# One buffer for the raw down weights of the first gated network, beside a ring of three for its up weights

## The chip, the cores and the metric

The kernel runs on one core of a Trainium2 chip. A core has a matrix engine (TensorE, "PE" in the profile; "PEld" is its weight load), a vector engine (VectorE, "DVE"), a scalar engine (ScalarE, "ACT"), a general engine (GpSimd, "POOL") and a queue processor (SyncE, "SP") that issues most of the transfers from main memory into the on-chip buffer. The engines run side by side, each works through its own instructions in order, and they wait for each other by semaphores. The metric is the device time of one execution in microseconds; lower is better.

## The reference

A decoder trunk of two layers on one sequence of 512 positions with 1024 channels, all in float32. The first layer mixes tokens with a state-space model, the second with attention. Behind each mixer stands a gated feed-forward network with 2816 hidden channels. Every sub-layer is preceded by a normalisation whose shift, scale and gate come from a conditioning vector `c` through a matrix `ada_w`. What matters here is the gated network:

```python
def conv_ffn(h, w_up, conv_w, conv_b, w_down):
    up = h @ w_up
    a, b = jnp.split(up, 2, axis=-1)
    S = a.shape[1]
    ap = jnp.pad(a, ((0, 0), (CONV_W - 1, 0), (0, 0)))
    a_conv = conv_b
    for i in range(CONV_W):
        a_conv = a_conv + ap[:, i:i + S] * conv_w[i]
    return (jax.nn.silu(a_conv) * b) @ w_down
```

With `h` 512 x 1024, `w_up` 1024 x 5632 and `w_down` 2816 x 1024. In `reference`, layer 0 calls `s5_mixer`, then `conv_ffn`; layer 1 calls `fox_mixer`, then `conv_ffn`; a last `rmsnorm` follows.

## The kernel before

Activations are kept transposed: channels on the 128 partitions, the 512 positions along the free axis. A float32 product is made from three products of halves: each operand is split into a high part and the remainder (`w_hi`, `w_lo` for weights), and TensorE computes hi·hi, hi·lo and lo·hi into the same accumulator (`mms`, L275). The split of a weight costs one ACT copy (`w_hi`, L258) and one DVE subtraction (`w_lo`, L259), both in `put_parts`.

A weight tile first lands in a buffer named `raw` (`raw()`, its transfer is issued on the SP queue at L167). These buffers are a ring of `RAW = 3`; a buffer is free again when ACT and DVE have read it. The `w_hi` and `w_lo` tiles are rings of `WB = 5`, free again when TensorE has used them.

The gated network (`ffn`) walks over 22 blocks `f` of 128 hidden channels. A block needs two up-weight tiles of 128 x 1024 (512 KB each). For most blocks of the first network `quarters` computes the up product with seven quarter products instead of eight (Strassen–Winograd): from the two raw tiles `a` and `b` it makes on DVE the sums `c` and `d` (L499), splits `a`, `c`, `d` (128 x 1024 each) and a quarter of `b`, called `a22` (128 x 512), and then runs 84 matmuls of 256 columns (`times`, L529), whose results ACT copies out (L536) and DVE combines (L499). A causal convolution (L578, L580), a SiLU (L583) and the gate product (L590) follow. Blocks 0, 1, 2, 3, 6, 11 and 17 (`plain`) take the ordinary product instead.

The blocks stand in five groups, (4, 4, 5, 4, 5). From the second group on, each block `f` is followed by one or two of the eight down products of the *previous* group (`down(q - 1, ...)`): each loads one raw tile of the down weights (128 x 512, 256 KB, for a group of four; 128 x 640, 320 KB, for a group of five), splits it, runs 12 or 15 matmuls of 512 columns, and adds the result into the residual `h` (L343). So a *step* of this loop loads `a` and `b`, then one or two down tiles, which the texts below call d1 and d2. There are 32 such down tiles, 14 pairs and 4 single ones. The eight down products of the last group follow behind the loop.

Beside that, the first gated network carries background work: the parameters of later sub-layers (`ada_units`), one transfer of 512 KB on the POOL queue and one DVE reduction (L228) for each unit, two units in most steps (`self.tick(ticks)`). The second gated network calls `ffn` with `ticks=0`: it has no such work.

The order of instructions on each engine, SP's transfers among them, is laid down when the program is built: a planner takes them in program order as operands and buffers come free in its own estimate of time, and the engines then keep to that order. Only the beginning of the state-space layer is ordered by hand (`manual_schedule`).

Pools of on-chip memory: `const` lives through the whole program; `s5p` lives through the state-space layer; `ffn0` and `ffn1` through the gated networks. `const` holds, among others, the pack `first` (the conditioning vector and small tables of the state-space layer, 176 floats to a partition) and `ones`, a 128 x 128 tile of ones. `ones` is the weight-side operand of the first normalisation (L1081), and one column of it is used in `rms_stats` (L361) throughout.

Of the kernel before, what the change touches and what calls it, by code (L numbers as in the profile page):

```python
# [8 lines left out]
F32 = mybir.dt.float32  # L9
F32R = mybir.dt.float32r  # L10
I32 = mybir.dt.int32
AF = mybir.ActivationFunctionType
# [5 lines left out]
P = 128  # L18
D = 1024
KT = D // P  # L20
# [22 lines left out]
FIRST = (("c", (KT,)), ("s5_prm", (3, G // 2)), ("s5_eye", (64,)), ("s5_causal", (L,)))  # L43
# [15 lines left out]
class Trunk:  # L59
# [6 lines left out]
    def __init__(self, tc, io, ctx):  # L66
        self.tc, self.nc, self.io, self.ctx = tc, tc.nc, io, ctx
        nc = self.nc
        pool = lambda name, bufs, **k: ctx.enter_context(tc.tile_pool(name=name, bufs=bufs, **k))
        self.const = pool("const", 1)  # L70
        self.act = pool("act", 1)
        self.wpool = pool("wpool", 3)
        self.tmp = pool("tmp", 2)
        self.small = pool("small", 2)
        self.dram = pool("dram", 1, space=DRAM)
        self.mm = pool("mm", 4, space=PSUM)
        self.aux = pool("aux", 4, space=PSUM)
        self.bg = []
        self.acc = None
        self.pending = None  # L80
        self.normed, self.evac, self.copied, self.squared = [], [], [], []
        self.sums = {}

        self.first = self.load_pack("first", FIRST)
        self.c = self.first["c"]
        self.ones = self.const.tile([P, P], F32, name="ones")
        nc.vector.memset(self.ones, 1.0)
        self.sc = self.const.tile([P, KT], F32, name="sc")
        nc.scalar.activation(self.sc, self.c, AF.Silu)
        self.scd = self.dram.tile([KT, P], F32, name="scd")  # L90

        self.sel = self.const.tile([P, 6], F32, name="sel")
        nc.gpsimd.memset(self.sel, 0.0)
        for q in range(4):
            for c in (q, 4 + q % 2):
                nc.gpsimd.memset(self.sel[32 * q:32 * q + 1, c:c + 1], 1.0)
        self.par = [self.const.tile([P, 24], F32, name=f"par{i}") for i in range(4)]
        self.ga = [self.const.tile([P, KT], F32, name=f"ga{i}") for i in range(4)]

    def load_pack(self, name, parts):  # L100

        t = self.const.tile([P, sum(math.prod(s) for _, s in parts)], F32, name=name)
        self.nc.sync.dma_start(t, self.io[name])
        out, a = {}, 0
        for n, s in parts:
            w = math.prod(s)
            v = t[:, a:a + w]
            out[n] = v.rearrange("p (a b) -> p a b", b=s[1]) if len(s) == 2 else v
            a += w
        return out  # L110

    def load_rest(self):
        for n, v in self.load_pack("rest", REST).items():
            setattr(self, n, v)

    def load_x(self, pool):
# [46 lines left out]
            yield  # L163

    def raw(self, shape, src, n=0):
        t = self.wpool.tile(shape, F32, name="raw", tag=("raw", "w_hi", "w_lo")[n], bufs=(RAW, WB, WB)[n])
        self.nc.sync.dma_start(t, src)  # L167
        return t
# [184 lines left out]
    def rms_stats(self, cols):  # L353

        nc = self.nc
        nb = (cols.stop - cols.start) // P
        parts = [t[:, cols] for t in (self.acc, self.acc_last)]
        ps = self.aux.tile([P, nb], F32, name="aux")
        for n, part in enumerate(parts):
            for b in range(nb):  # L360
                nc.tensor.matmul(  # L361
                    ps[:, b:b + 1], part[:, b * P:(b + 1) * P], self.ones[:, 0:1],
                    start=(n == 0 and b == 0), stop=(n == 1), skip_group_check=True,
                )
        return self.inv_root(ps, nb)
# [196 lines left out]
    def ffn(self, i, l, x, nxt, ticks=0, plain=None):  # L562

        nc, tc = self.nc, self.tc
        with tc.tile_pool(name=f"ffn{l}", bufs=1, reuse_waits="tile") as pool:
            self.bgpool = pool
            conv = pool.tile([P, 4, FT], F32, name="conv_wb")
            nc.sync.dma_start(conv, self.io["conv"][l])
            cw, cb = conv[:, :3], conv[:, 3]
            groups = QGROUPS[l] if plain else GROUPS  # L570
            first = [sum(groups[:q]) for q in range(len(groups) + 1)]
            keep, g = {}, {}

            def gated(m, ps, cols):
                f = m // 2
                if m % 2 == 0:
                    t = pool.tile([P, S], F32, name="conv", bufs=2 if plain else 3)
                    nc.scalar.activation(t, ps, AF.Identity, bias=cb[:, f:f + 1], scale=cw[:, 2, f:f + 1])  # L578
                    for d in (1, 2):
                        c = nc.vector.scalar_tensor_tensor(  # L580
                            t[:, d:], ps[:, :S - d], cw[:, 2 - d, f:f + 1], t[:, d:], op0=ALU.mult, op1=ALU.add
                        )
                    nc.scalar.activation(t, t, AF.Silu)  # L583
                    keep[f] = t
                    if plain and f >= groups[0]:
                        self.evac = [c.ins]
                        self.tick(ticks)
                    return
                t = keep.pop(f)
                nc.vector.tensor_tensor(t, t, ps, ALU.mult)  # L590
                q = sum(f >= n for n in first[1:])
                j = f - first[q]
                if not j:
                    tag = f"{q % 2}" if plain else ""
                    g[q] = [pool.tile([P, groups[q], S], F32R, name=n, tag=n + tag) for n in ("ghi", "glo")]
                hi, lo = g[q]
                self.put_parts(hi[:, j, :], lo[:, j, :], t)

            after, y = nxt
            up = lambda fs, **k: self.product(  # L600
                self.io["w_up"][l], range(2 * fs[0], 2 * fs[-1] + 2), KT, x, gated,
                ticks=0 if plain else ticks, **k
            )
            last = len(groups) - 1
            down = lambda q, ms, **k: self.product(
                self.io["w_down"][l][:, :, first[q]:first[q + 1], :], ms, groups[q], g[q],
                self.add_residual(i, q == last), after=after, ticks=0 if plain else ticks, **k
            )
            todo = []
            for q, n in enumerate(groups):  # L610
                fs = range(first[q], first[q + 1])
                if not plain:
                    up(fs, head=0 if q else 3)
                    if q < last:
                        down(q, range(KT))
                    continue
                for j, f in enumerate(fs):
                    if f == 0:
                        up([0, 1], head=3)
                        todo.append(self.forms_x(pool, x))  # L620
                    elif f in plain:
                        if f > 1:
                            up([f])
                        for _ in range(4):
                            if todo and next(todo[0], True):
                                todo.pop()
                    else:
                        while todo:
                            if next(todo[0], True):
                                todo.pop()  # L630
                        self.quarters(pool, l, f, x, gated)
                    if q:
                        down(q - 1, range(j * KT // n, (j + 1) * KT // n))
                        self.tick(ticks)
            down(last, range(KT), tail=TAIL if plain else 2, tail_pool=(pool, 4))
        return y
# [121 lines left out]
class S5(Trunk):  # L758
# [292 lines left out]
    def s5(self, i, nxt):  # L1051
        nc, tc = self.nc, self.tc
# [4 lines left out]
        with ExitStack() as stack:  # L1057
            spool = lambda name, st: st.enter_context(tc.tile_pool(name=name, bufs=1, reuse_waits="tile"))
            keep = spool("s5p", stack)
            self.s5q = spool("s5q", stack)  # L1060
            with ExitStack() as start:
                tp = spool("s5t", start)
# [10 lines left out]
                with tc.manual_schedule(engines={ENG.PE, ENG.Activation, ENG.DVE, ENG.SP}):  # L1073
# [4 lines left out]
                    for k in range(KT):  # L1078
                        sq = self.tmp.tile([P, S], F32, name="nm_t")
                        nc.scalar.activation(sq, self.h[:, k, :], AF.Square)  # L1080
                        nc.tensor.matmul(ps, self.ones, sq, start=(k == 0), stop=(k == KT - 1))  # L1081
                    rows = self.tmp.tile([P, S], F32, name="nm_t")
                    nc.scalar.activation(rows, ps, AF.Copy)
                    stats = self.aux.tile([P, NB, P], F32, name="aux")
# [527 lines left out]
```

## Time and profile before

| what | value |
|---|---|
| device time, median of 3 runs | 1247.41 us (1247.23 to 1250.16) |
| profiled execution: device time | 1250.96 us |
| profiled execution: span shown in the profile | 1249.2 us |
| TensorE busy, share of the span | 1217.2 us, 97% |
| VectorE busy | 1010.6 us, 81% |
| ScalarE busy | 609.2 us, 49% |
| bytes moved | 183.83 MB |

The span runs from the first to the last instruction of the profiled execution. "Busy" is the time in which an engine executes; a row of a view names the line of the code, the engine, the operation, the output and the inputs, and then durations. An arrow (`<-`) behind an idle time names what the engine was waiting for. The granted clock is the share of the full rate that TensorE was allowed in a stretch.

In the span the state-space layer takes about the first 260 us, the first gated network lies from about 265 to 635 us, attention to about 890 us and the second gated network behind it.

### The profile page before, as it was taken

What the parts mean: (1) busy time and instruction counts of PE and PEld (TensorE: products, weight loads), DVE (VectorE), ACT (ScalarE), POOL (GpSimd) and SP (SyncE); (2) the same over time, 40 slices, a digit from 0 to 9 for tenths busy, and PEclk for the clock granted to TensorE, in tenths of its full rate; (3) what the DMA queues carried; (4) which work ended last, traced back from release to release, by engine and by line L of the source; (5) the groups of instructions that cost most, each with busy time, mean ns of one, the idle gap of its engine ahead of it and who ended that gap; (6) DMA issues with size and microseconds to landing.
All of it is one profiled execution on the core that took longest, in us unless ns stands there. A gap on an engine that the chain in (4) does not pass through costs nothing.

```text
span 1249.2 us, 20558 instructions
## 1 busy us (share of the span) xinstructions
PE 1217.2 (97%) x7921; PEld 1039.6 (83%) x7921; DVE 1010.6 (81%) x1871; ACT 609.2 (49%) x1137; POOL 83.3 (7%) x143
## 2 busy tenths in 40 slices
PE   7999999999998999999999999999999999999997
PEld 2566678898988888889899877878989999999987
DVE  7888986779888888899788587885899887888855
ACT  3544465335444444444553565654366544555443
POOL 0000000100000000000000233431000000000000
PEclk9999989999998999999999999999999999999999
DMA  9677668521343544453525444432213332323331
GB/s 365 221 240 241 218 196 289 204 96 34 126 170 114 186 152 150 159 194 127 162 102 203 163 142 148 154 106 85 87 51 110 118 111 83 110 92 115 100 94 68
DMA packets 74385, 183.83 MB, mean 147 GB/s; under 512 B 23231, under 2 KB 25631, under 8 KB 73263
## 3 DMA queue, kind: packets, MB, share of 16 engines
q1 hardware_dynamic: 68239, 161.02, 38.1%
q0 software_dynamic: 5760, 20.97, 5.0%
q8 instruction: 62, 1.02, 0.3%
q10 hardware_dynamic: 288, 0.52, 0.1%
q14 instruction: 36, 0.29, 0.1%
HBM read 175.57 MB, written 6.92 MB: 146 GB/s over the span
## 4 chain that ended last, share of the span: by engine, by line
PE 70%; issue 14%; DVE 8%; DMA 5%; ACT 1%; POOL 1%; SPq 0%; DVEq 0%; POOLq 0%; ACTq 0%
PE mmp L275 29%; PE mmp L529 14%; PE aux L529 6%; PE mmp L1141 4%; PE mmp L1332 2%; DVE w_lo L259 2%; PE aux L947 2%; DMA raw<-in_w_up 2%; PE mmp L1170 2%; PE aux L1036 1%; PE aux L1471 1%; PE mmp L186 1%; PE aux L1028 1%; DVE ada_raw L228 1%; PE mmp L1081 1%
## 5 line engine op out<-in xcount | busy, mean ns | idle before, releaser
L258 ACT ACTIVATE w_hi<-raw 128x1024 fp32r<-128x1024 f32 (+5 forms) x205 | 175.9, 865 | 145.5 <-PE mmp L275 61.2
L259 DVE TENSOR_TENSOR w_lo<-raw,w_hi 128x1024 fp32r<-128x1024 f32 (+5 forms) x205 | 207.0, 1017 | 49.1 <-ACT w_hi L258 48.8
L275 PE MATMUL mmp<-ghi,w_hi 128*128 128x512 f32 (+1 forms) x392 | 146.4, 373 | 0.0
L275 PE MATMUL mmp<-glo,w_hi 128*128 128x512 f32 (+1 forms) x392 | 146.1, 373 | 0.0
L275 PE MATMUL mmp<-ghi,w_lo 128*128 128x512 f32 (+1 forms) x392 | 145.9, 372 | 0.0
L275 PE MATMUL mmp<-a_hi,w_hi 128*128 128x512 f32 (+1 forms) x376 | 139.0, 372 | 1.5 <-ACT a_hi L414 1.5
L275 PE MATMUL mmp<-a_hi,w_lo 128*128 128x512 f32 (+1 forms) x376 | 136.6, 364 | 0.0
L275 PE MATMUL mmp<-a_lo,w_hi 128*128 128x512 f32 (+1 forms) x376 | 136.4, 363 | 0.0
L529 PE MATMUL mmp<-w_hi,w_lo 128*128 128x256 f32 x396 | 111.9, 283 | 3.6 <-DVE w_lo L259 3.6
L529 PE MATMUL mmp<-w_hi 128*128 128x256 f32 x396 | 112.3, 284 | 2.8 <-ACT w_hi L258 2.1
L529 PE MATMUL mmp<-w_lo,w_hi 128*128 128x256 f32 x396 | 111.5, 282 | 0.0
L258 ACT ACTIVATE w_hi<-sums 128x1024 fp32r<-128x1024 f32 x74 | 77.5, 1057 | 32.9 <-DVE sums L499 31.4
L536 ACT ACTIVATE nm_h<-mmp 128x256 f32<-128x256 f32 x99 | 37.5, 381 | 111.3 <-PE mmp L529 111.0
L259 DVE TENSOR_TENSOR w_lo<-sums,w_hi 128x1024 fp32r<-128x1024 f32 x74 | 90.2, 1219 | 0.5 <-ACT w_hi L258 0.4
L275 PEld LDWEIGHTS mmp<-ghi,w_lo 128*128 128x128 f32 x392 | 73.9, 189 | 14.2
L343 DVE SCALAR_TENSOR_TENSOR h<-mmp,par,h 128x512 f32<-128x512 f32 (+1 forms) x100 | 68.2, 683 | 20.6 <-PE mmp L275 20.1
L275 PEld LDWEIGHTS mmp<-ghi,w_hi 128*128 128x128 f32 x392 | 74.0, 189 | 12.9
L275 PEld LDWEIGHTS mmp<-glo,w_hi 128*128 128x128 f32 x392 | 73.9, 189 | 12.8
L275 PEld LDWEIGHTS mmp<-a_hi,w_hi 128*128 128x128 f32 x376 | 70.5, 189 | 14.1 <-issue 2.6
L275 PEld LDWEIGHTS mmp<-a_hi,w_lo 128*128 128x128 f32 x376 | 70.9, 189 | 11.8 <-DVE w_lo L259 0.6
L529 PEld LDWEIGHTS mmp<-w_hi 128*128 128x128 f32 x396 | 76.4, 193 | 3.6 <-ACT w_hi L258 2.5
L275 PEld LDWEIGHTS mmp<-a_lo,w_hi 128*128 128x128 f32 x376 | 71.1, 189 | 9.9
(314 smaller groups left out, 3065.2 us busy)
## 6 DMA issues: line engine op xcount, KB each, us to landing
raw<-in_w_up SPq DMA_DIRECT2D x88, 512.0 KB, 3.5
raw<-in_ada_w SPq DMA_DIRECT2D x40, 512.0 KB, 6.1
ada_raw<-in_ada_t POOLq DMA_DIRECT2D x40, 512.0 KB, 4.0
raw<-in_w_down SPq DMA_DIRECT2D x32, 320.0 KB, 3.2
nf<-nfd SPq DMA_DIRECT2D x8, 1152.0 KB, 6.5
raw<-in_fox_qk SPq DMA_DIRECT2D x16, 512.0 KB, 3.8
raw<-in_w_down SPq DMA_DIRECT2D x24, 256.0 KB, 3.0
raw<-in_w_down SPq DMA_DIRECT2D x16, 384.0 KB, 3.3
```

The costliest lines, as they stand in the source:

```text
L186: self.last_mm = nc.tensor.matmul(ps[32 * qq:32 * qq + 32, :], self.sc32[:, k, :], w[:, q * S:(q + 1) * S], start=(step is steps[0]), stop ...
L228: nc.vector.tensor_tensor_reduce(w, w, self.c_row, 1.0, 0.0, ALU.mult, ALU.add, sums[:, j:j + 1])
L258: nc.scalar.activation(hi, src, AF.Copy)
L259: return nc.vector.tensor_tensor(lo, src, hi.bitcast(F32), ALU.subtract)
L275: self.last_mm = self.nc.tensor.matmul(o, wt, xt[:, cols], start=(k == 0 and n == 0), stop=(k == nk - 1 and n == 2),)
L343: add = self.nc.vector.scalar_tensor_tensor(self.h[:, m, cols], ps, self.par[i][:, 16 + m:17 + m], self.h[:, m, cols], op0=ALU.mult, op1=A ...
L529: self.last_mm = nc.tensor.matmul(o, wt[:, k], xt[:, k], start=(first and k == 0 and n == 0), stop=(k == H - 1 and n == 2), skip_group_che ...
L536: a = nc.scalar.activation(t, o, AF.Copy)
L947: nc.tensor.matmul(ps[g2][:, j, cols], x[rows, a + j, r].rearrange("p c j -> p (c j)"), self.rr[rows, planes, q, :], start=(j == 0 and r = ...
L1141: nc.tensor.matmul(ps, w[m][:, k, :], x[:, k], start=(k == 0), stop=(k == KT - 1))
L1170: nc.tensor.matmul(gps[m], wt, xt[:, k], start=(k == 0 and part == 0 and xt is yhi), stop=(k == KT - 1 and part == 1))
L1332: self.last_mm = nc.tensor.matmul(ps[q, b][:, :n], xt[:, k, tb], wt, start=(k == 0 and i == 0), stop=(k == KT - 1 and i == 2),)
```

## The change

While the loop of the first gated network issues a down product, `self.room` is set to `"rawd"`. `raw()` then takes the tile from the network's own pool under that name, with one buffer, instead of from the ring. The ring of three is left to the up weights in that loop. The last group's down products, which follow the loop, and the second gated network take the ring as before.

`rawd` takes 640 floats (2560 bytes) of each partition. The pack `first` and the 128 x 128 tile of ones move from `const`, which lives through the program, to `s5p`, the pool of the state-space layer. In `const` there stays a single column of ones, `one`, which `rms_stats` uses now. The load of `first` and the SiLU of `c` move with the pack, from the constructor to the beginning of `s5`.

```diff
@@ Trunk.__init__
-        self.first = self.load_pack("first", FIRST)
-        self.c = self.first["c"]
-        self.ones = self.const.tile([P, P], F32, name="ones")
-        nc.vector.memset(self.ones, 1.0)
+        self.room = None
+        self.one = self.const.tile([P, 1], F32, name="one")
+        nc.vector.memset(self.one, 1.0)
         self.sc = self.const.tile([P, KT], F32, name="sc")
-        nc.scalar.activation(self.sc, self.c, AF.Silu)
@@ load_pack, load_rest
-    def load_pack(self, name, parts):
-        t = self.const.tile([P, sum(math.prod(s) for _, s in parts)], F32, name=name)
+    def load_pack(self, name, parts, pool):
+        t = pool.tile([P, sum(math.prod(s) for _, s in parts)], F32, name=name)
         self.nc.sync.dma_start(t, self.io[name])
...
-        for n, v in self.load_pack("rest", REST).items():
+        for n, v in self.load_pack("rest", REST, self.const).items():
@@ raw
     def raw(self, shape, src, n=0):
+        if self.room:
+            t = self.bgpool.tile(shape, F32, name=self.room, bufs=1)
+            self.nc.sync.dma_start(t, src)
+            return t
         t = self.wpool.tile(shape, F32, name="raw", tag=("raw", "w_hi", "w_lo")[n], bufs=(RAW, WB, WB)[n])
@@ rms_stats
-                    ps[:, b:b + 1], part[:, b * P:(b + 1) * P], self.ones[:, 0:1],
+                    ps[:, b:b + 1], part[:, b * P:(b + 1) * P], self.one,
@@ ffn
                     if q:
+                        self.room = "rawd" if ticks else None
                         down(q - 1, range(j * KT // n, (j + 1) * KT // n))
+                        self.room = None
                         self.tick(ticks)
@@ s5
             keep = spool("s5p", stack)
+            self.first = self.load_pack("first", FIRST, keep)
+            nc.scalar.activation(self.sc, self.first["c"], AF.Silu)
+            ones = keep.tile([P, P], F32, name="s5_ones")
+            nc.vector.memset(ones, 1.0)
...
-                        nc.tensor.matmul(ps, self.ones, sq, start=(k == 0), stop=(k == KT - 1))
+                        nc.tensor.matmul(ps, ones, sq, start=(k == 0), stop=(k == KT - 1))
```

## The prediction, made before the result was known

> **What bounds the kernel now.** I read the page first, then the busy times by stretch, then who waits for whom on TensorE and VectorE, and last the transfers and the order of single instructions around the stalls. The page:
>
> ```profile
> span 1249.2 us, 20558 instructions
> PE 1217.2 (97%) x7921; PEld 1039.6 (83%) x7921; DVE 1010.6 (81%) x1871; ACT 609.2 (49%) x1137; POOL 83.3 (7%) x143
> ```
>
> TensorE is the bound as a whole, and all its idle time together is 32 us. A change that only moves weight transfers can win no more than what of that lies in the stage it touches, and what clock goes with it. So: the first gated network, in three stretches, with the loop of the second one for comparison (columns: stretch and its length, then busy time of PE, PEld, DVE, ACT, POOL, the granted clock, DMA share, GB/s):
>
> ```profile
> 240.00:375.00 135.00, 134.05 (x830) 119.91 (x829) 112.90 (x191) 61.85 (x94) 4.22 (x8) 1.00 0.34 120
> 375.00:525.00 150.00, 141.76 (x901) 128.56 (x900) 127.50 (x200) 66.61 (x107) 9.50 (x18) 0.97 0.45 150
> 525.00:620.00 95.00, 95.00 (x590) 84.94 (x589) 83.31 (x129) 48.07 (x74) 4.22 (x8) 1.00 0.51 169
> 925.00:1200.00 275.00, 275.00 (x1930) 255.89 (x1929) 231.04 (x342) 143.82 (x226) 0.00 (x0) 1.00 0.32 104
> ```
>
> Only 375 to 525 us has something to give: 150 − 141.76 = 8.2 us idle, and 3% of the clock, another 0.03 × 150 = 4.5 us; 12.7 us in all. Who ends the idle time in that stretch, for PE and then for DVE (total, times, longest):
>
> ```profile
> PE mmp L529 <- DVE w_lo L259: 3.6, 2, 2.8
> PE mmp L529 <- ACT w_hi L258: 2.1, 2, 1.2
> PE aux L529 <- DVE w_lo L259: 1.9, 1, 1.9
> PE mmp L529 <- ACT nm_h L536: 0.6, 2, 0.3
> ```
>
> ```profile
> DVE sums L499 <- DMA raw<-in_w_up: 9.9, 4, 3.9
> L259 DVE TENSOR_TENSOR w_lo<-raw,w_hi 128x1024 fp32r<-128x1024 f32 x10 | 12.2, 1222 | 6.1 <-ACT w_hi L258 6.1
> ```
>
> TensorE waits for split weights (7.6 of 8.2 us), and VectorE, which makes them, stands 9.9 us waiting for up weights to land and 6.1 us for the ACT copy of a raw up tile (the 128 x 1024 raw tiles are up weights). In three places this reaches TensorE:
>
> ```profile
> 390.00:410.00 20.00, 16.25 (x99) 15.21 (x99) 15.69 (x26) 8.66 (x15) 1.05 (x2) 0.83 0.41 144
> 415.00:430.00 15.00, 12.75 (x96) 11.87 (x95) 12.79 (x20) 7.29 (x11) 0.53 (x1) 1.00 0.47 158
> 495.00:505.00 10.00, 8.07 (x44) 7.25 (x43) 8.89 (x15) 4.21 (x7) 1.05 (x2) 0.83 0.24 71
> ```
>
> Stall A (390 to 410): 3.75 us idle and 0.17 × 20 = 3.4 us of clock. Stall B (415 to 430): 2.25 us, no clock. Stall C (495 to 505): 1.9 us idle and 0.17 × 10 = 1.7 us of clock.
>
> Ahead of A and C, VectorE stands still for a raw up tile that was sent for late:
>
> ```profile
> 386.10 0.33 SPq L167 DMA_DIRECT2D raw<-in_w_up  x1
> ```
>
> ```profile
> 390.88 0.69 DVE L499 TENSOR_TENSOR sums<-raw 128x512 f32<-128x512 f32 x1 [3.90 <-DMA raw<-in_w_up]
> ```
>
> ```profile
> 486.16 1.03 SPq L167 DMA_DIRECT2D raw<-in_w_up  x2
> ```
>
> ```profile
> 491.71 1.23 DVE L259 TENSOR_TENSOR w_lo<-raw,w_hi 128x1024 fp32r<-128x1024 f32 x1 [3.48 <-ACT w_hi L258]
> ```
>
> Why late? The four loads of a step share three buffers, and each is issued at the moment when VectorE has finished the previous owner. DVE, then SP, at the step behind stall A:
>
> ```profile
> 400.36 0.69 DVE L499 TENSOR_TENSOR sums<-raw,sums 128x512 f32<-128x512 f32 x1
> ...
> 402.95 0.68 DVE L259 TENSOR_TENSOR w_lo<-raw,w_hi 128x512 fp32r<-128x512 f32 x1
> ...
> 405.02 0.68 DVE L259 TENSOR_TENSOR w_lo<-raw,w_hi 128x512 fp32r<-128x512 f32 x1
> 405.93 0.69 DVE L259 TENSOR_TENSOR w_lo<-raw,w_hi 128x512 fp32r<-128x512 f32 x1 [0.23 <-ACT w_hi L258]
> ```
>
> ```profile
> 401.11 0.33 SPq L167 DMA_DIRECT2D raw<-in_w_down  x1
> 403.70 2.36 SPq L167 DMA_DIRECT2D raw<-in_w_up  x2
> 406.65 0.33 SPq L167 DMA_DIRECT2D raw<-in_w_down  x1
> ```
>
> The last sum frees `a` at 401.05, and the second down tile d2 goes out at 401.11. `a22` at 403.63 frees `b`, and the next `a` goes out at 403.70. The split of d1 ends at 405.70, and the next `b` goes out then. The split of d2 ends at 406.62, and the next d1 goes out at 406.65. A ring of three under four loads has no load ahead: every up tile is sent for when VectorE already has little else left of its step.
>
> **The change, part by part.** *The up tiles* keep the ring for themselves. At any step the ring holds `a`, `b` and the next `a`, which then lies there a whole step early. The next `b` follows when the last sum frees `a`: 401.05 in place of 405.70. In that step the split of a sum (1.22 us), `a22`, d1 and d2 still stand before VectorE, 3 us of work or more with the additions behind it, against this landing time (median us from issue to landing, the down tiles beside it):
>
> ```profile
> raw<-in_w_up SPq DMA_DIRECT2D x88, 512.0 KB, 3.5
> raw<-in_w_down SPq DMA_DIRECT2D x32, 320.0 KB, 3.2
> raw<-in_w_down SPq DMA_DIRECT2D x24, 256.0 KB, 3.0
> ```
>
> So the waits of 3.90 and 3.48 us go. They are longer than the idle of A (3.75) and C (1.9), so the stalls go with them, and their clock: 3.75 + 3.4 + 1.9 + 1.7 = 10.8 us. Stall B I leave standing: VectorE had no wait for an up tile ahead of it.
>
> [...] The rows: 0.83 over 20 us behind 3.75 us idle, 0.83 over 10 us behind 1.9 us, and 1.00 behind the 2.25 us of B. [...]
>
> *The down tiles* get one buffer. This is the new wait: d2 was sent for when `a` came free (401.05), and will now be sent for when d1 has been split (405.70): 4.65 us later at equal pace. Behind it on SP stand whatever up loads the planner places there. From the split of d1 to that of d2 it takes, for 256 KB, 3.0 us of landing, 0.6 us of ACT and 0.7 us of DVE: 4.3 us; for 320 KB 3.2 + 0.7 + 0.8 = 4.7 us:
>
> ```profile
> L258 ACT ACTIVATE w_hi<-raw 128x512 fp32r<-128x512 f32 x16 | 10.0, 625 | 14.8 <-DMA raw<-in_w_up 10.5 <-DMA raw<-in_w_down 4.2
> L258 ACT ACTIVATE w_hi<-raw 128x640 fp32r<-128x640 f32 x7 | 5.1, 730 | 1.6 <-DMA raw<-in_w_down 1.6
> L259 DVE TENSOR_TENSOR w_lo<-raw,w_hi 128x640 fp32r<-128x640 f32 x7 | 5.6, 819 | 1.0 <-ACT w_hi L258 1.0
> ```
>
> What covers it is TensorE's own work on d1, 5.60 / 2 = 2.8 us for 12 matmuls or 7.00 / 2 = 3.5 us for 15 (a pair of each, from the chain of waits), and the lead that d1 has:
>
> ```profile
> 457.74 5.60 PE mmp L275 x24
> ...
> 511.22 7.00 PE mmp L275 x30
> ```
>
> With no lead, a pair costs 4.3 − 2.8 = 1.5 us, or 4.7 − 3.5 = 1.2 us. There are 14 pairs, 10 of 256 KB and 4 of 320 KB: at worst 15 + 4.8 = 19.8 us. The lead today is seen here:
>
> ```profile
> 524.16 0.82 DVE L259 TENSOR_TENSOR w_lo<-raw,w_hi 128x640 fp32r<-128x640 f32 x1
> 527.40 0.83 DVE L259 TENSOR_TENSOR w_lo<-raw,w_hi 128x640 fp32r<-128x640 f32 x1 [2.42 <-ACT w_hi L258]
> ```
>
> ```profile
> 528.47 20.70 PE mmp L275 x90
> ```
>
> d1 is split at 524.98, d2 at 528.23, and TensorE begins with d1 at 528.47: a lead of 3.5 us. With 4.7 us between the two, d2 would be ready at 529.7, and it is needed at 528.47 + 3.5 = 532.0. So 2.3 us are left, and with VectorE's waits gone the lead grows. Between 0 and 19.8 us I take 1.5 us, one pair in 14, near the lower end because this row shows spare time.
>
> *The packs.* The load of `first` stays the first one on SP. One memset of a column is added on DVE beside that of `ones`, which took 0.165 us while VectorE waited for `first` to land anyway; the matmuls of L361 read a column at another place. Nothing of this is on the way to the end: 0, at worst the 0.2 us of one small DVE instruction at the start.
>
> **The sum.** 10.8 − 1.5 = 9.3 us. The profiled execution took 1250.96 us (span 1249.2), 3.55 us over the median of 1247.41. 1250.96 − 9.3 = 1241.7, and against the median 1238.1: I say 1238. The likeliest case's own range goes from all of the 12.7 us (1234.7) to half of the 9.3 (1242.8). Two runs of this kernel can be told apart from about 0.3%, 3.7 us.
>
> **The rivals.**
>
> *Nothing is won (1247).* SP takes its transfers in order. If the planner places the next `b` behind d2, it goes out when d1 has been split, at 405.70 in the rows above, which is when it goes out now; `a` alone comes early, and the sums on VectorE need `b` first. For it: that SP stands behind a single load for most of a step is the rule here, as this wait of its queue around 401 shows.
>
> ```profile
> SPq L167 <- DVE sums L499: 14.0, 1, 14.0
> ```
>
> A second way to the same end: VectorE's freed 16.0 us are filled with waits for d2, and TensorE is none the better. Against both: in 525 to 620 VectorE is 88% busy (83.31 of 95) and TensorE has no idle at all, so VectorE need not be free of waits; and without A and C the stretch of 150 us would be about 139 us with VectorE at 127.5, 92%. For it again: the second network runs the same ring of three at 84% (231.04 of 275) without a stall, so the ring alone isn't what stalls. Chance 0.22.
>
> *Slower (1255).* The one buffer makes d2 late in most steps. Place: the pairs of down tiles; price 1.5 or 1.2 us each; it decides where d1's lead at TensorE falls under those 1.5 us, and costs more than the 10.8 us won from the eighth pair on. If A and C go and 13 of 14 pairs pay, 9 × 1.5 + 4 × 1.2 = 18.3 us, that is +7.5 us: 1255. For it: VectorE is the second busiest engine and follows one order, so a `w_lo` of d2 placed too early holds up everything behind it; 2.42 us of such a wait stand in the row at 527.40. Against it: the leads of 3.5 us above. Chance 0.2. [...] No row of this trace shows a single room under a pair of loads.
>
> **How the numbers follow.** Faster as forecast 0.58; no change 0.22; slower 0.20. The range of 8 in 10 reaches from all of the 12.7 us (1234) over the case of no change to half-way into the slower one, 1252.
>
> **What would show it.** Right: in the first network's loop the DVE waits for raw up tiles (9.9 and 6.1 us) shrink to a few us, the stalls of 3.75 and 1.9 us are gone, the clock there is 1.00, and the waits behind down tiles grow without reaching TensorE. Wrong: PE waits at L275 for a `w_lo` or `w_hi` of a down tile (the slower rival); up loads on SP that stand behind a down load (no change); or a loss outside 240 to 640 us, which no step here accounts for.

## The result, and the profile after

| | before | changed |
|---|---|---|
| device time, median | 1249.82 us (11 runs) | 1243.50 us (11 runs) |
| profiled execution: device time | 1250.96 us | 1240.36 us |
| profiled execution: span | 1249.2 us | 1238.6 us |

The ratio of changed to before is 0.9948, with a 95% interval of 0.9930 to 0.9967: 6.3 us faster by the medians. Faster was forecast, with 1238 us from a median of 1247.41, a gain of 9.3 us. Two thirds of that came. One execution in the experiments below, of the kernel listed as "one room, split behind copies", took 4893.13 us at a granted clock of 0.233 and is left out of that kernel's median and ratio.

The page of the changed kernel, and the stretches of the first gated network (columns as in the prediction: length, busy time of PE, PEld, DVE, ACT, POOL, granted clock, DMA share, GB/s):

```profile
span 1238.6 us, 20567 instructions
PE 1209.1 (98%) x7921; PEld 1032.3 (83%) x7921; DVE 1008.9 (81%) x1872; ACT 606.4 (49%) x1137; POOL 82.3 (7%) x143
```

```profile
240.00:375.00 135.00, 133.45 (x828) 119.39 (x828) 115.79 (x194) 63.40 (x98) 4.06 (x8) 1.00 0.39 127
375.00:525.00 150.00, 148.51 (x967) 134.41 (x966) 131.56 (x209) 68.38 (x110) 10.03 (x19) 1.00 0.49 159
525.00:620.00 95.00, 91.12 (x588) 82.19 (x587) 79.92 (x125) 43.10 (x71) 3.69 (x7) 1.00 0.46 142
```

The stretch from 375 to 525 us did what was forecast: 1.5 us idle in place of 8.2, the clock at 1.00 in place of 0.97. The next stretch gave back: it had no idle time before and has 3.9 us now, 2.8 us of it in the loop and 1.1 us behind the loop, in the norm that follows (L363, at 619 us). Who waited in the whole first gated network, first for TensorE, then for ScalarE (total, times, longest), changed kernel:

```profile
PE mmp L531 <- ACT nm_h L538: 3.4, 2, 2.8
PE aux L363 <- DVE ssq L339: 1.4, 2, 1.1
PE mmp L531 <- DVE w_lo L261: 1.4, 2, 0.7
```

```profile
ACT w_hi L260 <- DMA rawd<-in_w_down: 34.3, 15, 5.7
ACT w_hi L260 <- DMA raw<-in_w_up: 7.3, 4, 3.2
ACT w_hi L260 <- DMA raw<-in_w_down: 4.9, 5, 1.7
```

And ScalarE before, in the same view:

```profile
ACT w_hi L258 <- DMA raw<-in_w_up: 35.3, 19, 4.9
ACT w_hi L258 <- DMA raw<-in_w_down: 15.5, 15, 3.1
```

The wait has changed its owner. ACT's waits for up tiles fell from 35.3 to 7.3 us; those for down tiles rose from 15.5 to 39.2 us, 34.3 us of it for the one buffer `rawd` (the room, from here on) and 4.9 us for the last group's tiles, which still take the ring. VectorE's 9.9 us of waiting for up tiles ahead of the sums (L499 before, L501 now) are gone from the list altogether.

The largest stall of TensorE in the loop is new and can be followed through the order of the instructions: DVE, SP, ACT (two rows), PE of the changed kernel, each with its start and length:

```profile
536.04 0.68 DVE L261 TENSOR_TENSOR w_lo<-rawd,w_hi 128x512 fp32r<-128x512 f32 x1
```

```profile
536.75 0.33 SPq L166 DMA_DIRECT2D rawd<-in_w_down  x1
```

```profile
540.82 0.63 ACT L260 ACTIVATE w_hi<-rawd 128x512 fp32r<-128x512 f32 x1 [4.03 <-DMA rawd<-in_w_down]
541.35 0.64 ACT L538 ACTIVATE nm_h<-mmp 128x256 f32<-128x256 f32 x2
```

```profile
541.77 0.39 PE L531 MATMUL mmp<-w_hi 128*128 128x256 f32 x1 [2.76 <-ACT nm_h L538]
```

The split of d1 ends at 536.72 and frees the one room. d2 is sent for at 536.75 and lands four microseconds later. Its `w_hi` stands first in ACT's order, so ACT does nothing for 4.03 us, and behind it stand two copies of finished quarter products. The first copy reads the accumulator to which TensorE adds its next product, so TensorE has to wait for it: 2.76 us idle. TensorE never waited for d2 itself; it waited for what stood behind d2 on ACT.

For the readings below it helps to have a length that holds the gated network alone. It runs from the first DVE convolution on an up product (its first start) to the first matmul of the attention's values (its first start). Before and changed:

```profile
L580 DVE SCALAR_TENSOR_TENSOR conv<-mmp,conv_wb,conv x22: 739/743/750, 290.6 to 933.3; 128x511 f32<-128x511 f32 x11, 128x510 f32<-128x510 f32 x11
...
L1332 PE MATMUL mmp<-w_hi,a_hi x112: 278/283/385, 639.2 to 686.9; 128*128 128x256 f32 x96, 128*128 128x272 f32 x16
```

```profile
L582 DVE SCALAR_TENSOR_TENSOR conv<-mmp,conv_wb,conv x22: 735/741/749, 287.9 to 922.8; 128x511 f32<-128x511 f32 x11, 128x510 f32<-128x510 f32 x11
...
L1340 PE MATMUL mmp<-w_hi,a_hi x112: 278/283/386, 629.2 to 676.8; 128*128 128x256 f32 x96, 128*128 128x272 f32 x16
```

639.2 − 290.6 = 348.6 us before, 629.2 − 287.9 = 341.3 us now. Of the 10.6 us between the two spans 7.3 lie here. 2.7 us lie ahead of it (290.6 against 287.9); whether they belong to the change, the kernel with the packs alone tells.

### The profile page after: what moved, and what is told of

It is laid out like the page before. It is cut to its first block, busy times and chain, and to the rows that moved or that the text cites. A ratio compares the mean times of both kernels' runs of the same rounds, so it can differ in the third digit from the quotient of the medians.

```text
span 1238.6 us, 20567 instructions
## 1 busy us (share of the span) xinstructions
PE 1209.1 (98%) x7921; PEld 1032.3 (83%) x7921; DVE 1008.9 (81%) x1872; ACT 606.4 (49%) x1137; POOL 82.3 (7%) x143
## 4 chain that ended last, share of the span: by engine, by line
PE 65%; issue 18%; DVE 10%; DMA 5%; ACT 2%; POOL 1%; SPq 0%; DVEq 0%; POOLq 0%; ACTq 0%
PE mmp L277 26%; PE mmp L531 12%; PE aux L531 5%; PE mmp L1149 4%; PE mmp L1340 3%; DVE w_lo L261 3%; DMA rawd<-in_w_down 2%; PE aux L951 2%; PE mmp L1178 2%; PE aux L1040 1%; PE aux L1479 1%; PE mmp L188 1%; PE aux L1032 1%; DVE ada_raw L230 1%; DMA ada_raw<-in_ada_t 1%
## 5 line engine op out<-in xcount | busy, mean ns | idle before, releaser
L261 DVE TENSOR_TENSOR w_lo<-raw,w_hi 128x1024 fp32r<-128x1024 f32 (+4 forms) x173 | 183.1, 1063 | 35.5 <-ACT w_hi L260 35.1
L260 ACT ACTIVATE w_hi<-raw 128x1024 fp32r<-128x1024 f32 (+4 forms) x173 | 154.6, 904 | 106.9 <-PE mmp L277 58.2
L538 ACT ACTIVATE nm_h<-mmp 128x256 f32<-128x256 f32 x99 | 37.7, 383 | 128.9 <-PE mmp L531 128.7
L260 ACT ACTIVATE w_hi<-sums 128x1024 fp32r<-128x1024 f32 x74 | 76.7, 1053 | 15.3 <-DVE sums L501 13.5
```

The costliest lines, as they stand in the source:

```text
L260: nc.scalar.activation(hi, src, AF.Copy)
L261: return nc.vector.tensor_tensor(lo, src, hi.bitcast(F32), ALU.subtract)
L538: a = nc.scalar.activation(t, o, AF.Copy)
```

## The experiments

My theory: the gain is that up tiles are no longer late; what was given back is the single room, by way of ACT's order. The rivals: the moved packs have a part in it; VectorE's load is the cause and not the ring; SP's order is.

All runs, in the order of the sections; "network" is the length just defined, in the run's profile; "clock" is the median of the granted clock over the executions of the run, and "span x clock" the median of their product, which takes most of the scatter of the clock out (an estimate, used beside the times and not for them; the kernel before reads 1238.4 to 1240.3 by it in the three groups of runs). The runs from "one room, loads doubled" on belong to the second group, those from "one room, split behind copies" on to the third:

| run | median us | ratio to before, interval | network us | clock | span x clock |
|---|---|---|---|---|---|
| before (first group) | 1250.12 | | 348.6 | 0.993 | 1239.7 |
| changed kernel | 1243.67 | 0.9952 (0.9928 to 0.9977) | 340.0 | 0.993 | 1233.5 |
| packs only | 1250.41 | 1.0003 (0.9982 to 1.0025) | 350.4 | 0.993 | 1239.8 |
| two rooms | 1236.30 | 0.9894 (0.9868 to 0.9920) | 336.5 | 0.996 | 1229.5 |
| down tiles on the POOL queue | 1243.24 | 0.9953 (0.9931 to 0.9975) | 343.2 | 0.994 | 1233.2 |
| before (second group) | 1248.98 | | | 0.992 | 1238.4 |
| one room, loads doubled | 1254.17 | 1.0045 (1.0018 to 1.0072) | 350.3 | 0.990 | 1241.3 |
| two rooms, loads doubled | 1236.72 | 0.9908 (0.9874 to 0.9943) | 334.0 | 0.993 | 1226.3 |
| no background, ring | 1233.73 | 0.9893 (0.9861 to 0.9925) | 332.9 | 0.996 | 1226.2 |
| no background, room | 1235.31 | 0.9900 (0.9871 to 0.9930) | 334.4 | 0.995 | 1226.6 |
| before (third group) | 1250.10 | | | 0.993 | 1240.3 |
| one room, split behind copies | 1237.89 | 0.9900 (0.9870 to 0.9929) | 335.5 | 0.994 | 1229.5 |
| two rooms, again | 1237.58 | 0.9905 (0.9876 to 0.9934) | 335.1 | 0.995 | 1229.4 |
| two rooms, split behind copies | 1234.19 | 0.9869 (0.9846 to 0.9892) | 333.2 | 0.996 | 1226.8 |
| two rooms, loads doubled, again | 1235.27 | 0.9891 (0.9866 to 0.9917) | 335.0 | 0.996 | 1228.9 |

### The changed kernel again, and the packs alone

The changed kernel, unedited:

> The changed kernel once more, as the measure for the other runs of this group. Every theory: 6 us under the kernel before (ratio 0.993 to 0.997), with the stall of 2.8 us at TensorE behind an ACT copy (L538) around 539 us.

Measured: 1243.67 us, ratio 0.9952. Its profile has the stall behind the copy again (2.4 us).

The packs alone:

```diff
-                        self.room = "rawd" if ticks else None
+                        self.room = None
```

> Only the packs move to the pool of the state-space layer; the down tiles stay in the ring of three. My theory, that the gain comes from the ring alone: as the kernel before, ratio 0.998 to 1.002, with TensorE idle 8 us between 375 and 525 us as there. The rival, that part of the gain lies ahead of the gated network (its first convolution starts 2.7 us earlier in the profile after): 2 to 3 us faster, ratio 0.998 or less, and the first convolution at 288 us and not at 290.6 us.

Measured: ratio 1.0003. The loop of this kernel is that of the kernel before, clock and all:

```profile
375.00:525.00 150.00, 142.21 (x911) 128.98 (x910) 125.03 (x198) 64.31 (x103) 9.50 (x18) 0.97 0.47 155
```

Its first convolution started at 287.4 us, earlier than in either of the other two, and it was no faster for it. The 2.7 us ahead of the network are clock. Between 150 and 200 us, in the state-space layer, the three profiles read (before, changed, packs alone):

```profile
150.00:200.00 50.00, 49.20 (x405) 39.41 (x402) 32.93 (x45) 26.70 (x56) 1.28 (x2) 0.93 0.71 237
```

```profile
150.00:200.00 50.00, 49.23 (x421) 39.11 (x414) 36.20 (x48) 29.70 (x60) 1.28 (x2) 1.00 0.74 243
```

```profile
150.00:200.00 50.00, 49.26 (x419) 39.48 (x416) 35.35 (x48) 28.68 (x58) 1.28 (x2) 1.00 0.75 243
```

By its row 0.07 × 50 = 3.5 us of clock were lost there in the profile before (an estimate). The last kernel below, two rooms with the split behind the copies, has the change in it, shows 0.93 there too, and starts its first convolution at 290.2 us. So the 2.7 us ahead of the network are not the change's. The packs cost and bring nothing that can be measured; the whole gain is the room's.

### A second room

```diff
         if self.room:
-            t = self.bgpool.tile(shape, F32, name=self.room, bufs=1)
+            self.turns = 1 - getattr(self, "turns", 1)
+            if self.turns and shape[1] <= 4:
+                t = self.tmp.tile(shape, F32, name="rawt", tag="ssq", bufs=1)
+            else:
+                t = self.bgpool.tile(shape, F32, name=self.room, bufs=1)
             self.nc.sync.dma_start(t, src)
```

The buffer of the squares (2 KB of a partition) is used only behind the loop, so no memory is added.

> The changed kernel with a second room for every other down tile of 128 x 512 (in the buffer of the squares, which stands empty in that loop); down tiles of 128 x 640 keep the one room. My theory, that the single room makes ACT wait for d2 and that this wait of 4.0 us held the copy that TensorE waited for: the stall of 2.8 us goes, ACT's wait for down tiles falls from 39 us to under 20 us, and the time is 2 to 4 us under the changed kernel (ratio to before 0.990 to 0.993). The rival, that VectorE's order is the cause and any late tile would do: the stall stays or moves, and the time is that of the changed kernel, within 1.5 us.

Measured: 1236.30 us, 7.4 us under the changed kernel in the same group, more than expected. TensorE no longer waits for a copy. TensorE, then ACT, in the gated network:

```profile
PE mmp L535 <- DVE w_lo L265: 1.5, 3, 0.7
```

```profile
ACT w_hi L264 <- DMA rawd<-in_w_down: 17.0, 5, 5.5
```

With the last group's 3.0 us, ACT waited 20.0 us for down tiles, against 37.1 us in the changed kernel of this group: nearly halved, where under 20 us was expected. By span x clock the step is 1233.5 − 1229.5 = 4.0 us; the rest of the 7.4 us goes with the higher clock (0.996 against 0.993). The second run of this kernel gave 1237.58 us.

### The down tiles on another queue

```diff
             t = self.bgpool.tile(shape, F32, name=self.room, bufs=1)
-            self.nc.sync.dma_start(t, src)
+            self.nc.gpsimd.dma_start(t, src)
```

> The changed kernel with the down tiles sent for on the POOL queue, so that on SP only up tiles are left and none can stand behind a down tile. If up tiles lose time behind down tiles on SP: ACT's remaining wait for up tiles (7.1 us) goes and the time falls by 1 to 2 us. My theory, that up tiles are no longer late: no gain from the queue; the landing of a down tile on the other queue takes longer, if at all, and the background transfers on the POOL queue stand behind the down tiles: same as the changed kernel or up to 5 us slower.

Measured: 1243.24 us, the changed kernel's time. ACT still waited 4.8 us for up tiles (6.6 us in the changed kernel of the same group), and for down tiles longer than there (32.3 us):

```profile
ACT w_hi L260 <- DMA rawd<-in_w_down: 45.9, 18, 5.2
PE aux L363 <- DVE ssq L339: 3.7, 2, 3.4
```

With no down tile of the loop on SP, most of the wait for up tiles is still there, so at most 1.8 us of it came from standing behind down tiles. The time by itself does not settle more than that: on the POOL queue the down tiles stand among the background transfers, and 3.4 us of TensorE's idle time lie in one wait behind the loop (L363), against 0.9 us in the changed kernel of this group. Why that wait grew was not followed.

### Loads doubled, with one room and with two

```diff
             self.nc.sync.dma_start(t, src)
+            self.nc.sync.dma_start(t, src)
             return t
```

One room:

> The changed kernel with each down tile loaded twice into the one room, one load behind the other, so that a down tile takes about 3.4 us longer. The slower rival of the prediction, priced: if d1's lead of 3.5 us is what keeps the single room harmless, the chain from d1 to d2 grows from 4.3 to about 7.7 us, over the cover of 2.8 us and the lead: 14 pairs at up to 3.4 us, 10 to 45 us slower than the changed kernel (1253 to 1288 us). If the leads are far longer than I read, or the planner makes room for it, under 3 us.

Measured: 1254.17 us, 10.5 us over the changed kernel of the first group (the kernel before read 1250.12 there and 1248.98 here). Now TensorE does wait for down tiles at L278, the line of the down products:

```profile
PE mmp L278 <- ACT w_hi L261: 5.6, 3, 3.0
PE mmp L532 <- ACT nm_h L539: 2.7, 2, 2.0
```

Three times, not 14: the leads are longer than I read in most pairs. The time is at the lower end of what was expected, and not all of it is wait at the down products: the clock from 375 to 620 us was 0.98, by estimate another 0.02 × 245 = 4.9 us.

Two rooms:

> The kernel with two rooms, again with each down tile loaded twice. If the price of a late down tile is the chain through one buffer, two rooms take most of it away: d2's loads run beside d1's, and only the tiles of 128 x 640 (one room, 4 pairs) still pay. Less than half of what the double load costs with one room; 0 to 12 us over the kernel with two rooms (1236 to 1248 us). If it is the landing time by itself that is late, whatever the buffer, as much as with one room.

Measured: 1236.72 us, and 1235.27 us when it was run again, against 1236.30 and 1237.58 us with single loads. The second time this was expected of it:

> Two rooms with each down tile loaded twice, again: in the profile it had less idle time at TensorE in the gated network (1.3 us against 3.1 us) than two rooms with single loads. If the planner, which takes the doubled load into its estimate, places the split of a down tile later and so keeps ACT free, the gain is real: 1 to 3 us under two rooms. If that was one execution's luck: the same within 1 us or slower.

With two rooms, a second load behind the first cost nothing. So what is dear about doubled loads in a single room is the chain through one buffer, not the landing time. (The planner takes the second load into its estimate and lays the order out anew, so the two kernels differ in more than the load.) Whether doubled loads are even better than single ones stays open: 1235.27 against 1237.58 us in one group, 1236.72 against 1236.30 us across groups.

### Without the background work

```diff
-        k.bg = [k.ada_units(units(*((2, t) for t in range(3)), (3, 2)))]
+        for t in (k.par[2], k.ga[2], k.par[3][:, 16:24]):
+            k.nc.gpsimd.memset(t, 0.5)
```

The kernel before with this edit:

> The kernel before without the background work of the first gated network: its 32 transfers of ada weights, their reductions on VectorE and the parameters made from them are left out (constants stand in their place). If VectorE's load (85% in the stretch of the stalls) is what turns a late up tile into a stall of TensorE, the stalls go though the down tiles share the ring: TensorE idle under 2 us between 375 and 525 us, 8 to 13 us faster than before (ratio 0.990 to 0.994). If late up tiles stall TensorE by themselves, the stalls stay: within 4 us of the kernel before.

Measured: ratio 0.9893. This kernel and the next leave out the parameters that the background work makes. All four loads of a step share the ring of three, and TensorE has no idle time from 375 to 525 us:

```profile
375.00:525.00 150.00, 150.00 (x988) 136.78 (x987) 120.64 (x180) 75.47 (x118) 0.00 (x0) 1.00 0.32 105
```

The changed kernel with this edit:

> The changed kernel without that background work (left out as in the run beside it). If the ring alone only hurts under VectorE's load, the room brings nothing here: within 2 us of the run beside it without the room; slower than it by what the single room costs when VectorE has time, which I expect at 0 to 2 us. If the room pays whatever VectorE has to do, 6 us faster than the run beside it.

Measured: 1235.31 us, 1.6 us over the run beside it, with overlapping intervals; by span x clock 0.4 us. So the ring of three under four loads does not stall TensorE by itself, and without the background work the room has nothing to mend. The reason is not that VectorE catches up behind late tiles: without the background work the up tiles are hardly late. ACT waited 3.7 us for them in the network, in place of 35.3 us:

```profile
ACT w_hi L258 <- DMA raw<-in_w_up: 3.7, 7, 1.2
```

The median time from issue to landing of an up tile, from 300 to 620 us, with the background work and without it:

```profile
raw<-in_w_up SPq DMA_DIRECT2D x35, 512.0 KB, 4.1
```

```profile
raw<-in_w_up SPq DMA_DIRECT2D x35, 512.0 KB, 3.3
```

So the edit took away two things at once: work of VectorE (127.5 us of 150 busy before, 120.6 now), which frees the buffers, and 32 transfers of 512 KB. Which of the two made the up tiles late is not shown. What is shown is that either the room or leaving out the background work removes the stalls of 375 to 525 us; whether a tile as late as before would stall a lighter VectorE was not tested.

### ACT's order

```diff
-        self.put_parts(hi, lo, self.raw(shape, src))
+        with self.behind(*(self.copied if self.room else ())):
+            self.put_parts(hi, lo, self.raw(shape, src))
```

`self.copied` is the third copy (L538) of the last quarter products; the edit lets no `w_hi` of a down tile stand ahead of it on ACT. One room:

> The changed kernel, one room, with the split of each down tile placed on ACT behind the third copy (L538) of the same block's quarter products. If it is ACT's order, a copy standing behind a w_hi that waits for its tile, that makes the single room cost something: the stall of TensorE behind a copy (2.4 to 2.8 us) goes without a second buffer, and the time is 2 to 5 us under the changed kernel (ratio 0.990 to 0.994). If the down tile is simply too late: TensorE waits for it at L277 instead, and the time is that of the changed kernel or up to 5 us more.

Measured: 1237.89 us, 5.8 us under the changed kernel of the first group (the kernel before read 1250.12 and 1250.10 us in the two), 4.0 us by span x clock: about as much as the second room brings. TensorE's wait behind a copy is gone, with the same single buffer:

```profile
PE mmp L532 <- ACT w_hi L261: 1.2, 2, 0.9
```

```profile
ACT w_hi L261 <- DMA rawd<-in_w_down: 21.3, 14, 3.3
```

TensorE waits for no down tile at L278 either, so the other outcome that was expected did not come. That settles what the single room cost: d2 was not too late for TensorE; its `w_hi` was too early in ACT's order. (The edit binds ACT's order alone; the planner then lays out the other engines around it, as in every kernel here.) Two rooms as the measure, and two rooms with this order:

> The kernel with two rooms once more, as the measure for this group: ratio 0.987 to 0.992 to the kernel before, 4 to 8 us under the changed kernel.

> Two rooms and the split placed behind the third copy. With two rooms hardly a copy stands behind a late tile, so there is little left to win: within 2 us of the kernel with two rooms. If down tiles, placed later, now come too late for TensorE: 2 to 6 us slower than it.

Measured: 1237.58 us, and 1234.19 us with the order, 3.4 us less, where under 2 us were expected. The intervals of the two ratios overlap. In the loop of the last kernel nothing is left to take:

```profile
290.00:610.00 320.00, 320.00 (x2018) 288.00 (x2017) 288.02 (x438) 156.37 (x246) 16.37 (x31) 1.00 0.48 152
```

It has the lowest median of the kernels that do all of the work: ratio 0.9869 to the kernel before (0.9846 to 0.9892), 15.9 us.

## Why the prediction was right, and where it was not

**The up tiles.** Right. The waits of VectorE for up tiles went, stalls A and C went, and packs alone brought nothing. The network is 7.3 us shorter in the profile. One rival stands untested: that a fourth buffer in the ring, shared by all loads, would have done the same. The runs show that the down tiles' own buffer helps, not that it has to be their own.

**Stall B.** "I leave standing" was wrong: it went too (1.5 us idle are left in 375 to 525 us). With the ring to themselves the up tiles come earlier for the planner as well, and the sums may then stand earlier in VectorE's order; that this is how B went was only argued.

**One pair in 14, 1.5 us.** This is the term that was mis-sized. The single room cost 4.0 us by span x clock, 5.8 to 7.4 us by medians: so much came back when either the second room or the order on ACT was put in. The price was worked out at the wrong place. It asked whether d2 reaches TensorE in time, by d1's lead. That part held: TensorE waited at no down product in the changed kernel, and only when the loads were doubled did it wait there, three times. What was not asked is what stands behind d2's `w_hi` on ACT while the tile is on its way. The prediction named the queue behind the waiting transfer (SP) and, among the rivals, a `w_lo` that holds up VectorE; the engine that was held up was the third one, ACT, which looked harmless at 49% busy.

**The clock.** 5.1 of the 10.8 us were clock behind A and C. In the profiles it came (0.97 to 1.00 in the loop). In the medians it did not: the granted clock over the whole span is 0.993 for both kernels, and the 6.3 us are a difference at equal clock (1239.7 − 1233.5 = 6.2 us). The kernels with two rooms, with the order on ACT or without background work have 0.993 to 0.996. A new stall that takes the clock where the old ones did would fit that, but the two profiles of the changed kernel speak against it: their clock is 1.00 around the new stall too (columns as above, the profile after):

```profile
530.00:550.00 20.00, 17.24 (x116) 15.70 (x115) 17.81 (x28) 10.20 (x17) 1.05 (x2) 1.00 0.53 173
```

Both were executions of 0.996 and 0.997; none near the median of 0.993 was profiled, so where the clock is lost in those stays open.

**The sum.** That 9.3 us came as near to 6.3 us as it did is in part luck. If the kernel with two rooms is taken as the change without the price of the single room, the gain is 1250.12 − 1236.30 = 13.8 us by the medians and 10.2 us at equal clock, and the price 7.4 and 4.0 us, in place of 10.8 and 1.5 us. Gain and price were both put too low by the medians, and the two errors pull opposite ways. At equal clock 10.8 us is nearly right, but not for its reason: 5.1 us of it were clock, and stall B was not in it. The last kernel, free of every stall in the loop, is 1240.3 − 1226.8 = 13.5 us better at equal clock (1240.3 us is the kernel before in its group). That is what taking the stalls away brought at that measure, and the prediction's 8.2 us of idle time were short of it. The changed kernel takes 6.2 us of it.

**The packs.** 0 was right: 1.0003.

**"Nothing is won."** Ruled out by the result. Its reason, up tiles behind d2 on SP, is worth at most the 1.8 us of ACT's wait that went with the POOL queue. Its hint that the second network runs the same ring without a stall was sound: without background work, the other thing that the second network lacks, the first network does too.

**"Slower".** Its mechanism, one buffer under a pair, is real, and its direction shows once the loads are doubled (1.0045). Its deciding point was that d1's lead falls short; even then TensorE waited at a down product in 3 places only. Here the single room beat the shared ring by 6.3 us, and the second room brought about as much again (7.4 us), as did the order on ACT without one (5.8 us). So a second buffer was worth having in this kernel, and a single room of its own still beat a place in a fuller ring.

## What to carry to other kernels

When buffers are shared by loads of different urgency, look for the moment at which each load is issued: if it is always the end of the previous owner, the ring gives no look-ahead, and taking one kind of load out can pay: 6.3 us here, and nothing once the background work was gone. When a wait is moved, list what stands behind the waiting instruction on *every* engine that touches the tile, idle ones too: an engine at 49% that stands for 4 us in front of a copy stopped the one at 98%. And a placement behind the copies was worth about as much as a second buffer, and cost no memory.

## What the runs showed of the hardware that was not expected

The granted clock differed from one execution to the next of the same kernel: 0.988 to 0.997 over 12 executions of the changed kernel, 1248.39 us and 1239.83 us. Span x clock of the same executions stays within 1231.6 to 1234.9. So most of the 8.6 us of scatter is clock, and a term of the clock read off one profile is not one of the median; nor are 3.7 us enough to tell two single runs apart, as the prediction took it. Where in the span the clock fell differed from profile to profile too: the stretch of 150 to 200 us above read 0.93 in the profile before and 1.00 in two others. What decides that was not shown. The length of the idle time alone did not decide where the clock fell: it was 0.83 around the 1.9 us of idle in stall C, and stayed at 1.00 around the 2.25 us of stall B and the 2.76 us of the new stall.

TensorE's idle time understated here what the stalls cost. In the profile before, the loop shows 8.2 us idle and, as an estimate from its rows of the clock, 4.5 us of clock (5.1 us by the two short stretches of A and C), 12.7 to 13.3 us. The network of the last kernel, which has no stall in the loop, is 623.4 − 290.2 = 333.2 us, 15.4 us shorter:

```profile
L587 DVE SCALAR_TENSOR_TENSOR conv<-mmp,conv_wb,conv x22: 739/742/750, 290.2 to 918.1; 128x511 f32<-128x511 f32 x11, 128x510 f32<-128x510 f32 x11
...
L1345 PE MATMUL mmp<-w_hi,a_hi x112: 278/283/387, 623.4 to 670.9; 128*128 128x256 f32 x96, 128*128 128x272 f32 x16
```

In the profile before, a matmul of 256 columns is shown as 0.28 us long (282 to 284 ns at L529), and 24 of them in a row took 2.81 us, so one started every 2.81 / 24 = 0.12 us:

```profile
463.34 2.81 PE mmp L529 x24
```

So by these two figures a start that comes up to 0.28 − 0.12 = 0.16 us late would show as no idle time (an estimate). That the remaining 2.1 to 2.7 us are such gaps was not shown.
